# A streaming encoder step: the last 272 queries of each head as tiles of 128, 72 and 72 instead of 128, 128 and 16

## Chip, cores and metric

One core of a Trainium2 chip runs the whole step as one program. The metric is the time of one execution on the device in microseconds (us). Three runs of the kernel before took 1683.66, 1681.59 and 1683.21 us, median 1683.21. A further execution was recorded by the profiler; the rows below come from it.

## What is computed

A layer with two head groups over 2064 prompt positions (16 learned meta tokens and 2048 tokens) and a small decoding batch: normalisation, one input projection, attention with forgetting in 8 heads of 64, a gated convolution, an output projection and a last normalisation. The change touches the prompt's attention only:

```python
def fox_block(qblk, cq, qpos, k, v, ck, kpos):
    s = jnp.einsum('bqhd,bkhd->bhqk', qblk, k, preferred_element_type=jnp.float32) * (DH ** -0.5)
    s = s + jnp.transpose(cq, (0, 2, 1))[..., None] - jnp.transpose(ck, (0, 2, 1))[:, :, None, :]
    mask = kpos[None, :] <= qpos[:, None]
    s = jnp.where(mask[None, None], s, -jnp.inf)
    p = jax.nn.softmax(s, axis=-1)
    return jnp.einsum('bhqk,bkhd->bqhd', p.astype(v.dtype), v)
```

All inputs and outputs are 32-bit floats; products are made of a high and a low part of each factor.

## The kernel before

The prompt is worked in two groups of positions: 1280 first, then the other 784. For each group the kernel normalises, projects, and runs attention interleaved with projections (`ps` tiles from `hh`, `hl` and the weights `wh`, `wl`, or `wvh`, `wvl` for values) and with the convolution. At the end comes the output projection.

Attention goes by head and by unit. A unit is 256 queries, `u` from 0 to 7; units 5, 6 and 7 belong to the second group. The last one, `u` = 7, has 272 queries, since 2064 is 16 more than 8 times 256. `query_tiles` gives the query tiles of a unit as (first query, number, keys seen). A unit has three stages, each written as a generator:

- `scores_of`: for each query tile and each chunk of up to 512 keys two matmuls into `sp` (`kb,qb` with 68 rows of contraction, `ka,qa` with 128), for the last chunk a third that adds the causal mask; VectorE copies `sp` to `s` and takes the row maximum, ScalarE takes the exponential in place and the row sum into `nm`, VectorE its reciprocal.
- `weights_of`: for each block of 128 keys the weights `s` are transposed on TensorE into `tp`, one matmul per query tile with the tile's weights as the stationary and an identity as the moving operand. So a tile of 16 queries has 16 rows of contraction and 16 moving columns. ScalarE copies `tp` to `ph`, VectorE writes the rest to `pl`. `tp` has two buffers, `ph` and `pl` three. A unit of 272 has 17 key blocks: fifteen are seen by all tiles, the sixteenth by two, the last (16 keys) by one.
- `values_of`: per key block two products, `ph,vb` and `pl,vb`, into `o`; at the unit's end the reciprocals in `nm` are transposed into `tr` in the same way, one matmul per query tile, and the result is scaled and gated.

All instructions go through `Queue.call` (line 278), which notes an estimated cost in `Times`; all rows therefore carry line 278. `Times.weave` chooses, by these estimates, which generator goes on next, and this fixes the order of TensorE. On VectorE, ScalarE, GpSimd and SyncE `settle` sorts the instructions by estimated start. A transpose is booked at 109 ns whatever its columns (`cost`). `vb`, the values of a head, has one buffer; its load in `load_values` can begin when the head before has made its last product. Loads are issued on SyncE's queue (SP), stores on GpSimd's.

Of the kernel before, what the change touches and what calls it, by code (L numbers as in the profile page):

```python
# [18 lines left out]
DRAM = bass.MemoryType.DRAM  # L19

P = 128
# [11 lines left out]
NPOS = SEQ + NMETA  # L33
# [281 lines left out]
class Step:  # L315
# [4 lines left out]
        for k, v in args.items():  # L320
            setattr(self, k, v)

    def dma(self, out, in_):

        if out.dtype == F32R:
            out = out.bitcast(F32)
        if in_.dtype == F32R:
            in_ = in_.bitcast(F32)
        return getattr(self.nc, STORES if out.space == DRAM else "sync").dma_start(out=out, in_=in_)

    def open(self, ctx, name, side=None, space=None):
        k = {}
# [47 lines left out]
    def load_constants(self, pool):  # L380
        nc, dma = self.nc, self.dma
        mraw = pool.tile([P, P], F32, name="mraw")
        dma(out=mraw, in_=self.cst[:, C_MASK:C_MASK + P])
        nc.vector.tensor_copy(out=self.mask, in_=mraw)
        for i in range(3):
            dma(out=self.cw[:, :, i], in_=self.conv_w[0, i].rearrange("(c p) -> p c", p=P))

        nc.vector.tensor_scalar(out=self.cw, in0=self.cw, scalar1=0.5, scalar2=None, op0=ALU.mult)
# [22 lines left out]
    def normalise(self, ph, xp, bufs, beside=()):  # L411
# [7 lines left out]
        def prepare():  # L419
            i, (pos, rows, ct, col) = todo.pop(0)  # L420
            xt = xp.tile([P, D], F32, name="xt", bufs=bufs)
            if pos == 0:
                dma(out=xt[:NMETA], in_=self.meta_tokens)
                dma(out=xt[NMETA:], in_=self.x_p[:P - NMETA])
            else:
                dma(out=xt[:rows], in_=self.x_s if pos == NPOS else self.x_p[pos - NMETA:pos - NMETA + rows])
            if pos == p0:
                dma(out=g_bc, in_=self.norm_g[0].partition_broadcast(P))
            if beside:
                beside.pop(0)()  # L430
            sq = xp.tile([P, D], BF16, name="sq")
            ss = xp.tile([P, 1], F32, name="ss", bufs=4)
            nc.scalar.activation(out=sq[:rows], in_=xt[:rows], func=AF.Square, accum_out=ss[:rows])
            self.rsqrt(ss[:rows])
            nc.vector.scalar_tensor_tensor(out=xt[:rows], in0=xt[:rows], scalar=ss[:rows, 0:1], in1=g_bc[:rows],
                                           op0=ALU.mult, op1=ALU.mult)
            ahead.append((xt, rows, ct, col, i))
# [486 lines left out]
    @staticmethod  # L924
    def query_tiles(u):

        out = [(0, P, 256 * u + P), (P, P, 256 * u + 256)]
        return out + [(256, 16, NPOS)] if u == 7 else out

    @staticmethod  # L930
    def unit_queries(u):
# [33 lines left out]
    def scores_of(self, ph, st, ready):  # L965

        nc = self.nc
        units = st["units"]
        loaded, asked = 0, 0
        while ph not in self.summed:  # L970
            yield lambda: 0.0 if ph in self.summed else NEVER
        for n, (h, u) in enumerate(units):
            while ("q", h // 2) not in ready:
                yield lambda: 0.0 if ("q", h // 2) in ready else NEVER

            for ahead in range(2):
                if loaded < H and loaded <= h + ahead and ("k", loaded // 2) in ready:
                    self.load_head(ph, loaded)
                    loaded += 1
                if asked < len(units) and asked <= n + ahead and ("q", units[asked][0] // 2) in ready:  # L980
                    self.load_queries(ph, asked, st)
                    asked += 1
            qa, qb, ka, kb = self.qa[n % 2], self.qb[n % 2], self.ka[h % 2], self.kb[h % 2]
            done = []
            for c0, m, nk in self.query_tiles(u):
                while st["tiles"] - st["turned"] >= SB[ph]:
                    yield lambda: 0.0 if st["tiles"] - st["turned"] < SB[ph] else NEVER
                st["tiles"] += 1
                sl = self.ap.tile([P, min(self.nk, NPOS)], F32, name="s", bufs=SB[ph])
                mx = self.ap.tile([P, 8], F32, name="nm", bufs=16)  # L990
                blocks = (nk + P - 1) // P
                nch = (nk + 511) // 512
                ends = [min(nk, (blocks * (x + 1) // nch) * P) for x in range(nch)]
                k0 = 0
                for x, k1 in enumerate(ends):
                    w = k1 - k0
                    yield self.when(qa, qb, ka, kb, slot=(self.sps, "sp"))
                    sp = self.sps.tile([P, 512], F32, name="sp", bufs=SPB)
                    diag = k1 == nk
                    nc.tensor.matmul(sp[:m, :w], qb[:, c0:c0 + m], kb[:, k0:k1], start=True, stop=False)  # L1000
                    nc.tensor.matmul(sp[:m, :w], qa[:, c0:c0 + m], ka[:, k0:k1], start=False, stop=not diag)
                    if diag:
                        nc.tensor.matmul(sp[:m, w - m:w], self.identr[:, :m], self.mask[:, :m], start=False, stop=True)
                    nc.vector.tensor_scalar(out=sl[:m, k0:k1], in0=sp[:m, :w], scalar1=1.0, scalar2=None, op0=ALU.mult,
                                            op1=ALU.max, accum_out=mx[:m, x:x + 1])
                    k0 = k1
                nm = mx[:, 6:8]
                nc.vector.tensor_reduce(out=nm[:m, 0:1], in_=mx[:m, :nch], axis=AX.X, op=ALU.max, negate=True)
                nc.scalar.activation(out=sl[:m, :nk], in_=sl[:m, :nk], func=AF.Exp, bias=nm[:m, 0:1], accum_out=nm[:m, 1:2])
                nc.vector.reciprocal(out=nm[:m, 1:2], in_=nm[:m, 1:2])  # L1010
                done.append((sl, nm))
            st["scored"].append(done)
# [548 lines left out]
STORES = "gpsimd"  # L1561
# [77 lines left out]
```

## Time and profile before

| | us |
|---|---|
| median of three runs | 1683.21 |
| profiled execution | 1680.57 |
| its span in the trace | 1678.7 |
| TensorE (PE) busy | 1564.9 |
| VectorE (DVE) busy | 861.0 |
| ScalarE (ACT) busy | 632.5 |
| GpSimd (POOL) busy | 481.2 |

Times in rows are us from the span's start, durations us unless marked ns. A row of a timeline gives start, duration, engine and instruction; consecutive instructions of one kind on one tile are merged into one row with a count, under the shape of the first of them. For TensorE `16*128` are rows and columns of the stationary operand and `16x16` the moving one. TensorE's durations overlap, so the distance between two starts, not the duration, tells how long an instruction held the engine. PEld is the weight load.

### The profile page before, as it was taken

Reading aid. Unit: us, or ns where it says so; the run is one execution under the profiler, and the core shown is the slowest. Engines: PE = TensorE matmul, PEld = TensorE weight load, DVE = VectorE, ACT = ScalarE, POOL = GpSimd, SP = SyncE. Lnnn points to the kernel's source line nnn. Section 1 sums busy time; section 2 is a strip of 40 time slices with the busy share of each in tenths; the row PEclk is TensorE's granted clock in tenths of the full one; section 3 lists DMA queues with packets and bytes.
Section 4 is the critical chain, followed back from the end, with each engine's and each line's share of the span. In section 5 each row is a group of like instructions: output and inputs, shape, how many; then the busy total and the mean of one; then the engine's idle time right before and its main releaser. Section 6 shows DMA issues by size and latency. Waiting matters only on the chain.

```text
span 1678.7 us, 27726 instructions
## 1 busy us (share of the span) xinstructions
PE 1564.9 (93%) x10311; PEld 1452.5 (87%) x10311; DVE 861.0 (51%) x2276; ACT 632.5 (38%) x1196; POOL 481.2 (29%) x750
## 2 busy tenths in 40 slices
PE   4789999998999989899995999999999999999996
PEld 4779999998999978899984998998898999868885
DVE  4525667336667557552332666776576673212221
ACT  4314555325553322411111655555554553111221
POOL 2543435523211421225041313212121121223322
PEclk9899999999999998999997999999999999999998
DMA  7446653475432676522237534535534231364442
GB/s 193 118 120 158 155 142 111 113 191 139 105 77 55 219 222 194 153 53 76 40 83 155 137 101 125 127 92 158 140 67 114 37 85 31 88 232 135 142 138 88
DMA packets 159143, 206.06 MB, mean 123 GB/s; under 512 B 22220, under 2 KB 123108, under 8 KB 156320
## 3 DMA queue, kind: packets, MB, share of 16 engines
q1 hardware_dynamic: 73952, 106.38, 22.2%
q10 hardware_dynamic: 61360, 30.94, 11.9%
q0 software_dynamic: 23696, 66.96, 11.5%
q8 instruction: 82, 1.34, 0.3%
q14 instruction: 53, 0.43, 0.1%
HBM read 137.28 MB, written 66.93 MB: 122 GB/s over the span
## 4 chain that ended last, share of the span: by engine, by line
PE 73%; DMA 11%; issue 6%; POOL 3%; DVE 3%; ACT 2%; SPq 1%; ACTq 0%; POOLq 0%; DVEq 0%
PE ps L278 45%; PE sp L278 10%; PE o L278 9%; PE tp L278 8%; DMA raw<-in_w_in_dram 3%; PE tr L278 1%; DMA sqk_d<-el 1%; DMA vb<-v_d 1%; SPq L278 1%; DMA qb<-ql_d 1%; DMA cat_d<-kf 1%; DMA vn<-in_cache_v_dram 1%; DMA gz_d<-kf 1%; DMA o_d<-ol 1%; DMA xt<-in_x_prompt_dram 1%
## 5 line engine op out<-in xcount | busy, mean ns | idle before, releaser
L278 PE MATMUL ps<-hh,wh 128*128 128x256 f32 (+2 forms) x1568 | 502.0, 320 | 20.1 <-DVE el L278 10.0
L278 PE MATMUL ps<-hl,wh 128*128 128x256 f32 (+2 forms) x1568 | 486.3, 310 | 0.0
L278 PE MATMUL ps<-hh,wl 128*128 128x256 f32 (+2 forms) x1568 | 485.9, 310 | 0.0
L278 PEld LDWEIGHTS ps<-hh,wh 128*128 128x128 f32 x1568 | 302.8, 193 | 29.6 <-DVE el L278 10.6
L278 PEld LDWEIGHTS ps<-hl,wh 128*128 128x128 f32 x1568 | 302.6, 193 | 1.6
L278 PEld LDWEIGHTS ps<-hh,wl 128*128 128x128 f32 x1568 | 301.6, 192 | 0.0
L278 DVE TENSOR_TENSOR pl<-tp,ph 128x512 fp32r<-128x512 f32 (+2 forms) x360 | 198.2, 564 | 113.2 <-ACT ph L278 111.3
L278 ACT CAST ph<-tp 128x512 fp32r<-128x512 f32 (+2 forms) x360 | 170.8, 487 | 210.3 <-PE tp L278 197.3
L278 DVE TENSOR_SCALAR_CACHE_REDUCE s<-sp 128x384 f32<-128x384 f32 (+3 forms) x360 | 210.5, 598 | 35.1 <-PE sp L278 33.5
L278 ACT ACTIVATE s<-s,nm 128x128 f32<-128x128 f32 (+16 forms) x136 | 170.5, 1254 | 77.6 <-DVE nm L278 77.0
L278 PE MATMUL tp<-ident,s 128*128 128x128 f32 (+1 forms) x1224 | 191.8, 269 | 0.1
L278 PE MATMUL o<-ph,vb 128*128 128x256 f32 (+4 forms) x584 | 167.6, 306 | 3.4 <-DMA vb<-v_d 3.4
L278 PEld LDWEIGHTS tp<-ident,s 128*128 128x128 f32 (+1 forms) x1224 | 145.0, 140 | 23.9 <-issue 19.9
L278 PE MATMUL sp<-kb,qb 68*128 68x384 f32 (+3 forms) x360 | 143.2, 398 | 18.4 <-DVE s L278 10.8
L278 PE MATMUL o<-pl,vb 128*128 128x256 f32 (+4 forms) x584 | 149.6, 282 | 0.0
L278 PE MATMUL sp<-ka,qa 128*128 128x384 f32 (+3 forms) x360 | 132.7, 369 | 0.0
L278 POOL TENSOR_TENSOR gz<-gz,otmp 64x256 f32<-64x256 f32 (+1 forms) x64 | 47.2, 737 | 273.2 <-DVE otmp L278 253.7
L278 PE MATMUL ps<-o,ch 128*128 128x512 f32 x374 | 118.6, 396 | 2.0 <-DMA o<-o_d 2.0
L278 PEld LDWEIGHTS o<-ph,vb 128*128 128x128 f32 (+1 forms) x584 | 109.9, 188 | 9.1 <-DMA vb<-v_d 2.4
L278 PEld LDWEIGHTS o<-pl,vb 128*128 128x128 f32 (+1 forms) x584 | 110.5, 189 | 0.7
L278 DVE TENSOR_TENSOR wl<-raw,wh 128x1024 fp32r<-128x1024 f32 x56 | 69.0, 1232 | 63.1 <-ACT wh L278 62.4
L278 PE MATMUL ps<-wvh,hh 128*128 128x272 f32 (+3 forms) x288 | 87.2, 303 | 5.0 <-ACT sv L278 4.6
(218 smaller groups left out, 2288.2 us busy)
## 6 DMA issues: line engine op xcount, KB each, us to landing
raw<-in_w_in_dram ACTq DMA_DIRECT2D x59, 512.0 KB
cr<-cat_d SPq DMA_DIRECT2D x17, 512.0 KB
v_d<-vv POOLq DMA_DIRECT2D x32, 256.0 KB, 2.7
vb<-v_d SPq DMA_DIRECT2D x8, 1024.0 KB
oxt<-in_x_prompt_dram SPq DMA_DIRECT2D x16, 512.0 KB
out_dram<-oxt POOLq DMA_DIRECT2D x16, 512.0 KB, 2.9
xt<-in_x_prompt_dram SPq DMA_DIRECT2D x15, 512.0 KB
qa<-qh_d SPq DMA_DIRECT2D x112, 64.0 KB
```

What stands on the lines that cost most here:

```text
L278: r = f(*a, **k)
```

## The change

`query_tiles` cuts the queries of unit 7 into 128, 72 and 72. The second tile begins at query 1920 and sees 2048 keys, the third begins at 1992 and sees all 2064. Since the second tile no longer ends where its keys end, the mask matmul is given the columns from the tile's first query to the end of the chunk. `dma` gets an optional argument that nothing uses.

```diff
-    def dma(self, out, in_):
+    def dma(self, out, in_, by=None):
...
-        out = [(0, P, 256 * u + P), (P, P, 256 * u + 256)]
-        return out + [(256, 16, NPOS)] if u == 7 else out
+        if u == 7:
+            return [(0, P, 256 * u + P), (P, 72, 256 * u + 256), (200, 72, NPOS)]
+        return [(0, P, 256 * u + P), (P, P, 256 * u + 256)]
...
-                        nc.tensor.matmul(sp[:m, w - m:w], self.identr[:, :m], self.mask[:, :m], start=False, stop=True)
+                        b0 = 256 * u + c0
+                        nc.tensor.matmul(sp[:m, b0 - k0:w], self.identr[:, :m], self.mask[:, :k1 - b0], start=False, stop=True)
```

The order on TensorE in the first unit of 272, two key blocks and the start of the next; the shapes here are those of the result, partitions by columns. Before:

```order
L278 MATMUL tp<-ident,s 128x128 x2
L278 MATMUL tp<-ident,s 128x16
L278 MATMUL o<-ph,vb 128x272
L278 MATMUL o<-pl,vb 128x272
L278 MATMUL tp<-ident,s 128x128 x2
L278 MATMUL tp<-ident,s 128x16
```

And after:

```order
L278 MATMUL tp<-ident,s 128x128
L278 MATMUL tp<-ident,s 128x72 x2
L278 MATMUL o<-ph,vb 128x272
L278 MATMUL o<-pl,vb 128x272
L278 MATMUL tp<-ident,s 128x128
L278 MATMUL tp<-ident,s 128x72 x2
```

Nothing moved: each group keeps its three transposes and its place, and the widths are others. The end of the same unit, the last three key blocks, before:

```order
L278 MATMUL ps<-hh_7939,wl 128x256
L278 MATMUL tp<-ident,s 128x128 x2
L278 MATMUL tp<-ident,s 128x16
L278 MATMUL tp<-ident,s 128x128
L278 MATMUL tp<-ident,s 128x16
L278 MATMUL tp<-ident,s 16x16
L278 MATMUL sp<-kb_9563,qb_9568 128x512
```

And after:

```order
L278 MATMUL ps<-hh_7939,wl 128x256
L278 MATMUL tp<-ident,s 128x128
L278 MATMUL tp<-ident,s 128x72 x4
L278 MATMUL tp<-ident,s 16x72
L278 MATMUL sp<-kb_9563,qb_9568 128x512
```

Six transposes stand there as before, one of 128 and five of 72 columns where three of 128 and three of 16 were. SyncE's queue (SP) at the beginning of the last head, where the values `vb` (in two pieces) and the queries of the next unit (`qa`, `qb`) are loaded:

```order
+L278 DMA vb<-v_d_109 128x2048
 L278 DMA vb<-v_d_109 16x128
-L278 DMA qa_9566<-qh_d_95 64x272 x2
+L278 DMA qa_9566<-qh_d_95 64x272
+L278 DMA qb_9568<-c_d 1x2x128
+L278 DMA qa_9566<-qh_d_95 64x272
 L278 DMA qb_9568<-ql_d_99 64x272
-L278 DMA qb_9568<-c_d 1x2x128
-L278 DMA vb<-v_d_109 128x2048
 L278 DMA qb_9568<-c_d 1x2x128
```

The large piece of `vb` moved from behind four of the five query loads to the front.

## Rows read from the trace of the kernel before

**Rows 1.** The page, part 1: busy us, share of span, instructions per engine.

```profile
PE 1564.9 (93%) x10311; PEld 1452.5 (87%) x10311; DVE 861.0 (51%) x2276; ACT 632.5 (38%) x1196; POOL 481.2 (29%) x750
```

**Rows 2.** Busy times by stretch; columns as in the first line.

```profile
core 0: us, PE busy (x) PEld busy (x) DVE busy (x) ACT busy (x) POOL busy (x), PEclk, DMA share, GB/s
...
930.00:1170.00 240.00, 239.92 (x1736) 216.84 (x1735) 162.25 (x467) 130.83 (x239) 64.04 (x102) 1.00 0.45 118
1170.00:1405.00 235.00, 233.71 (x1695) 211.97 (x1694) 154.81 (x429) 121.38 (x218) 36.59 (x53) 1.00 0.38 87
```

**Rows 3.** Weight loads by shape: busy us, mean ns, idle before and its releaser.

```profile
L278 PEld LDWEIGHTS tp<-ident,s 16*128 16x128 f32 x128 | 17.1, 133 | 21.0 <-issue 19.9 <-ACT wvh L278 0.2
```

**Rows 4.** Timeline of TensorE, unit 7 of the second head: start, us, instruction.

```profile
1028.83 0.54 PE L278 MATMUL tp<-ident,s 128*128 128x128 f32 x3
1029.30 0.40 PE L278 MATMUL o<-ph,vb 128*128 128x272 f32 x1
1029.54 0.29 PE L278 MATMUL o<-pl,vb 128*128 128x272 f32 x1
...
1030.85 0.38 PE L278 MATMUL tp<-ident,s 128*128 128x128 f32 x2
```

**Rows 5.** The same group in narrower windows: from its second, its third transpose on.

```profile
1028.94 0.43 PE L278 MATMUL tp<-ident,s 128*128 128x128 f32 x2
...
1029.14 0.23 PE L278 MATMUL tp<-ident,s 16*128 16x16 f32 x1
```

**Rows 6.** Timeline of TensorE in a unit of 256 queries.

```profile
1044.54 0.61 PE L278 MATMUL tp<-ident,s 128*128 128x128 f32 x4
...
1045.11 0.29 PE L278 MATMUL o<-pl,vb 128*128 128x256 f32 x1
```

**Rows 7.** Timeline of TensorE, four transposes of 16 rows in a row.

```profile
719.18 0.41 PE L278 MATMUL sp<-ident,xt 16*128 16x16 f32 x4
719.53 0.38 PE L278 MATMUL ps<-hh,wh 128*128 128x256 f32 x1
```

**Rows 8.** Timeline of TensorE around a score matmul of 68 rows.

```profile
1012.00 0.34 PE L278 MATMUL sp<-kb,qb 68*16 68x384 f32 x1
1012.17 0.34 PE L278 MATMUL sp<-ka,qa 128*16 128x384 f32 x1
1012.35 0.28 PE L278 MATMUL ps<-wvh,hh 128*128 128x256 f32 x1
```

**Rows 9.** Timeline of TensorE: three runs of transposes and what follows them.

```profile
1017.72 1.08 PE L278 MATMUL tp<-ident,s 128*128 128x128 f32 x6
...
1018.95 0.28 PE L278 MATMUL ps<-wvl,hh 128*128 128x256 f32 x1
...
1033.70 0.99 PE L278 MATMUL tp<-ident,s 128*128 128x128 f32 x6
...
1034.96 0.40 PE L278 MATMUL sp<-ka,qa 128*128 128x512 f32 x1
...
1037.37 0.59 PE L278 MATMUL tr<-ident,nm 128*128 128x128 f32 x3
...
1038.23 0.40 PE L278 MATMUL sp<-ka,qa 128*128 128x512 f32 x1
```

**Rows 10.** Timelines of SP's issues and TensorE, start of the last head.

```profile
1348.41 0.31 SPq L278 DMA_DIRECT2D vb<-v_d  x1
...
1352.08 0.40 SPq L278 DMA_DIRECT2D vb<-v_d  x1
...
1358.02 0.36 PE L278 MATMUL o<-ph,vb 128*128 128x256 f32 x1 [1.09 <-DMA vb<-v_d]
```

**Rows 11.** Timelines of ScalarE and VectorE: copies of the group in rows 4.

```profile
1029.41 0.39 ACT L278 CAST ph<-tp 128x272 fp32r<-128x272 f32 x1 [0.80 <-PE tp L278]
...
1029.83 0.44 DVE L278 TENSOR_TENSOR pl<-tp,ph 128x272 fp32r<-128x272 f32 x1 [0.74 <-ACT ph L278]
```

More of the change, by code (lines that the diff above doesn't have):

```diff
@@ L328, in dma @@
             in_ = in_.bitcast(F32)
-        return getattr(self.nc, STORES if out.space == DRAM else "sync").dma_start(out=out, in_=in_)
+        return getattr(self.nc, by or (STORES if out.space == DRAM else "sync")).dma_start(out=out, in_=in_)
     def open(self, ctx, name, side=None, space=None):
```

## Prediction

> **What bounds the kernel now.** I read the busy shares first, then the stretch in which the changed code runs, then single rows of TensorE there, because a share says nothing about how fast an engine that is always busy could go. TensorE is busy 93% of the span [rows 1]. The units of 272 queries run between 930 and 1405 us, eight of them, one per head. In that stretch TensorE is busy 239.92 of 240 us and 233.71 of 235 us at the full granted clock (1.00, the level of 2.4 GHz), while VectorE is busy for about two thirds and ScalarE for about half [rows 2]. So a microsecond of TensorE taken out of this stretch comes off the span until another engine's result is late.
>
> What TensorE does badly there shows in the weight loads: the 128 loads with 16 rows stand behind 21.0 us of idle time, nearly all of it put down to "issue", that is, to no other engine [rows 3]. One group of three transposes shows it in order. It starts at 1028.83; the second transpose starts at 1028.94 (0.11 later), the third, with 16 rows, at 1029.14 (0.20 later), the first product `o` at 1029.30 (0.16 later), the second at 1029.54 [rows 4, 5]. From the first transpose to the second product: 0.71 us. In a unit without a 16-row tile, four transposes of 128 start at 1044.54 and the second product at 1045.11 [rows 6]: 0.57 us for one transpose more. Three steps of 0.109 (the 0.11 above, finer: 0.327 for three) leave 0.24 from the last transpose to the second product; the same stretch after a 16-row transpose is 0.40. Thus the 16-row tile costs on the way in, in itself and on the way out.
>
> Is that the price of 16 rows, or of changing to them? Four transposes of 16 rows in a row start at 719.18 and the next instruction at 719.53 [rows 7]. Take the 0.16 of the way out off these 0.35 us and three steps remain, of about 0.063 each (an estimate from these rows). So 16-row transposes are quick among themselves; the change of row count is what costs. That each of these loads 128 columns of weights also says that such a load needs no more than 0.063 us.
>
> The question is then on which side 72 rows fall. The scores have a neighbour: the matmul `sp<-kb,qb` has 68 rows and stands between matmuls of 128 rows. Its successor starts 0.17 us after it, and that one's successor 0.18 us after that, at the same 384 columns [rows 8]. No price for 68 rows on either side. I take 72 rows to behave like 68.
>
> **The change, part by part.** *Scores.* The number of score matmuls, their columns, the reductions on VectorE and the exponentials on ScalarE are the same; partitions are exchanged (128 and 16 against 72 and 72), columns are not. The mask matmul of the last tile grows from 16 to 72 columns, and the two products of the last key block do so too; with the steps of 0.109 for 128 columns as bound, each under 0.05 us, in sum under 0.15 a head. I take 0.07.
>
> *Transposes.* After the change a group is one of 128 columns (0.109) and two of 72. By columns a 72 would take 72/128 of 0.109, or 0.061; I take 0.063, the step seen above. After the last one the second product follows in 0.24 less the 0.046 by which 72 columns are shorter, 0.20 with the 16 columns more of `o`. Sum 0.109 + 0.063 + 0.20 = 0.37 against 0.71: 0.34 saved. Twelve groups of a head stand like this: 4.1 us.
>
> The other five groups of a head stand in two runs. The two triples from 1017.72 to the second matmul behind them at 1018.95 take 1.23 us; after the change 0.109 + 0.063 + 0.063 + 0.109 + 0.063 + 0.20 = 0.61, saved 0.62. The run of six from 1033.70 to 1034.96 takes 1.26 us and ends with a score matmul of 512 columns in place of 256, some 0.11 longer; after the change 0.109 + four times 0.063 + 0.30 = 0.66, saved 0.60. The three transposes of the denominators, 1037.37 to 1038.23, take 0.86 us; after it 0.109 + 0.063 + 0.30 = 0.47, saved 0.39 [rows 9]. The 16-row products of the last key block stay as they are.
>
> A head saves 4.1 + 0.62 + 0.60 + 0.39 - 0.07 = 5.6 us, eight heads 45 us.
>
> *Order.* The planner books every transpose at 109 ns whatever its columns, so around the groups its order stands still; small other costs move, and from behind the first unit of 272 on it shifts projections and scores by a few rows. The work of a head stays the same. One move has a price in the trace: in the last head the large load of `vb` now goes out ahead of four issues for `qa`/`qb`, where before it followed them, 1348.41 to 1352.08, and TensorE waited 1.09 us for it at 1358.02 [rows 10]. I credit 1 us. The other way, loads of `ka`/`kb` (five or six issues) now precede some of `qa`/`qb` in SP's queue; at 0.4 to 0.6 us an issue that is up to 3 us later for loads that are asked for one unit, some 15 us, ahead: hidden, and at most 3 us a head if not.
>
> *New waits.* `tp` has two buffers, so group j+2 may not start before VectorE has written `pl` of group j. Now ScalarE's copy starts 0.58 us after the group (1029.41), takes 0.39, VectorE's part starts 0.03 later and takes 0.44 [rows 11]: 1.44 in all; after the change the group itself is 0.14 shorter up to its last transpose (0.17 against 0.31), so 1.30, and some 0.05 for the signal. TensorE needs from group j to j+2 now 2.02 us (1028.83 to 1030.85, [rows 4]); after it 2.02 - 0.68 = 1.34. The two are equal within the reading. Where VectorE or ScalarE has something else in hand, of 0.4 us or so, the wait shows. About six such pairs a head, 48 in all: between 0 and 48 times 0.3, 14 us. I take 5 us, nearer the lower end, because the units of 128-row tiles in the same stretch run with the same two buffers and TensorE stays busy through them [rows 2].
>
> Together 45 + 1 - 5 = 41 us off. The profiled execution took 1680.57 us, its span 1678.7; I expect a span near 1638. The median of the runs is 2.6 us above the profiled one: 1683.2 - 41 = **1642 us**.
>
> **The rivals.** *A transpose of 72 columns keeps the pace of one of 128.* Then each of the 35 in a head (33 of weights, two of denominators) costs 0.046 more, 13 us in eight heads, and fewer waits appear: about 1653. The four 16-row ones [rows 7] speak against it. The Trainium skill's page "TensorE: Matmul & The Clock Gate", section "LDWEIGHTS (loading the stationary operand)", has a rule for this: loading takes the stationary columns divided by 1.2 GHz, whatever the rows. For 128 columns that is an estimate of 107 ns by that page, which would keep every transpose at the pace of 128 and give this rival's time; by it 16 rows would also cost nothing extra, and the trace has 0.063 us for such a load and 0.20 plus 0.16 around it, so the trace disagrees.
>
> *The waits decide.* If `pl` is late by 0.3 us or more at each pair because VectorE's order blocks it, the 14 us above and more are lost: 1652 to 1665.
>
> *72 rows count as another row count.* Entering costs 0.20, the second 72 follows at 0.063, leaving costs 0.40: 0.66 against 0.71, 0.05 saved some 128 times (the transposes of 16 rows, [rows 3]): about 1677. The change would then not do what its form suggests. The 68-row matmul [rows 8] speaks against it. The same skill's page "TensorEngine Tiling (Array Packing)", section "Tiling Modes", lists modes of 128, 64 and 32 rows and says that a change of mode drains the engine; 16 rows fit the mode of 32, and 72 fit only that of 128. By that rule this rival falls; the trace agrees for 68 rows.
>
> *Slower: every 72-row tile pays for itself.* If each step into and between 72-row transposes cost 0.20, a group would take 0.20 + 0.20 + 0.40 = 0.80 against 0.71, and 128 times 0.09 are 12 us: about 1695. It decides as soon as the step from 72 to 72 exceeds 0.11. No row has 72 rows; the quick run of four [rows 7] speaks against it.
>
> **How the numbers follow.** My forecast, 1634 to 1650 around 1642, has 0.80. The pace rival has 0.08, the waits 0.05, the rival of another row count 0.03, the slower one 0.04. The range reaches from all of the gain without a wait and with a slightly quicker 72 (1634) to the waits at their price (1660); beyond it lie the last two and a part of the waits. A measurement of this kernel can tell some 0.2% (3.4 us) from no change: faster 0.95, same 0.01, slower 0.04.
>
> **What would show it.** Right: from the first transpose of a group to the second product 0.37 us; the idle time put down to "issue" before weight loads of `tp` nearly gone; no row of 16 rows but those of the last key block; some 5 us per head less between the units' ends; TensorE still busy nearly throughout, with a few new waits on `pl`. Wrong: steps of 0.11 between transposes of 72 (pace), waits on `pl` or `ph` of more than 10 us in sum (waits), a gap of 0.20 ahead of each 72 (row count).

## The result, and the profile after

The changed kernel takes 1657.76 us (median of four, 1652.27 to 1664.70) against 1682.40 us of the kernel before in the same session: 0.9868 of it, 95% interval 0.9836 to 0.9900, so 24.6 us faster. The prediction had said 41 us faster. The direction holds, the size does not. The profiled execution after took 1664.70 us and its span is 1662.9; it is the slowest of the four and already 6.1 us behind the profiled execution before when the first changed instruction comes, so parts are compared below by their own lengths and not by their place on the clock.

The steps on TensorE came nearly as the sum had them. A group of the second head (timeline, first from its first transpose, then two narrower windows, as in [rows 4, 5]; start, us, instruction):

```profile
1038.00 0.40 PE L278 MATMUL tp<-ident,s 128*128 128x128 f32 x3
1038.20 0.37 PE L278 MATMUL o<-ph,vb 128*128 128x272 f32 x1
1038.41 0.29 PE L278 MATMUL o<-pl,vb 128*128 128x272 f32 x1
1038.53 0.27 PE L278 MATMUL tp<-ident,s 128*128 128x128 f32 x1
...
1038.11 0.29 PE L278 MATMUL tp<-ident,s 72*128 72x72 f32 x2
...
1038.17 0.23 PE L278 MATMUL tp<-ident,s 72*128 72x72 f32 x1
```

From 128 to 72 columns 0.11, from 72 to 72 0.06 to 0.07, from the last transpose to the first product 0.03 and to the second 0.24: 0.41 from the first transpose to the second product, where [rows 4] has 0.71. The weight loads of `tp` by shape (busy us, mean ns, idle before and its releaser) answer [rows 3]:

```profile
L278 PEld LDWEIGHTS tp<-ident,s 128*128 128x128 f32 x960 | 115.3, 142 | 13.3 <-DVE pl L278 10.0
L278 PEld LDWEIGHTS tp<-ident,s 72*128 72x128 f32 x256 | 32.5, 146 | 1.1 <-ACT s L278 1.1
```

The idle time put down to "issue", 19.9 of the 21.0 us in [rows 3], is gone. In its place the loads of 128 rows wait 10.0 us for VectorE's `pl`, where in the kernel before all loads of `tp` wait 0.3 us for it (waits: us in total, times, longest):

```profile
PEld tp L278 <- DVE pl L278: 0.3, 1, 0.3
```

The stretch of the units of 272 shows the same by its busy times (columns as in [rows 2]; x counts instructions):

```profile
936.00:1170.00 234.00, 226.66 (x1731) 215.54 (x1731) 160.84 (x463) 128.49 (x237) 63.57 (x103) 0.98 0.46 121
1170.00:1400.00 230.00, 225.12 (x1760) 215.90 (x1759) 161.07 (x446) 124.87 (x226) 37.46 (x54) 0.99 0.38 89
```

TensorE was without work for 0.08 and 1.29 us in [rows 2]; now it is for 7.34 and 4.88 us, and the granted clock is not full any more. What the weight loads waited for most in that stretch, and what ScalarE and VectorE themselves waited for among transfers:

```profile
PEld tp L278 <- DVE pl L278: 10.0, 6, 2.8
...
PEld ps L278 <- DVE kf L278: 1.7, 1, 1.7
...
ACT kf L278 <- DMA cat_d<-kf: 4.8, 1, 4.8
...
ACT ph L278 <- DMA kb<-kh_d: 4.2, 1, 4.2
ACT wvh L278 <- DMA raw<-in_w_in_dram: 3.5, 1, 3.5
...
ACT kf L278 <- DMA kb<-c_d: 1.8, 1, 1.8
...
ACT wh L278 <- DMA raw<-in_w_in_dram: 1.7, 1, 1.7
...
DVE vv L278 <- DMA v_d<-vv: 4.2, 1, 4.2
```

In the kernel before, neither ScalarE nor VectorE has a single wait on a transfer between 930 and 1405 us. Here they stand six times from the first unit of 272 on, 20.2 us in sum. (Just ahead of it ScalarE stands for the store `gz_d` in both kernels: 6.1 us before, 5.0 us after.) The longest wait of TensorE in the stretch shows how one of them travels. Timelines of SP, GpSimd, VectorE and TensorE, second head:

```profile
1021.73 0.50 SPq L278 DMA_DIRECT2D ka<-kh_d  x1
...
1022.93 0.45 SPq L278 DMA_DIRECT2D ka<-kl_d  x1
1023.42 0.60 SPq L278 DMA_DIRECT2D kb<-kh_d  x1
...
1023.06 0.76 POOL L278 DMA_DIRECT2D v_d<-vv  x1
...
1032.88 0.23 DVE L278 CAST vv<-sv 128x128 fp32r<-128x128 f32 x1 [4.20 <-DMA v_d<-vv]
1033.03 0.43 DVE L278 TENSOR_TENSOR pl<-tp,ph 128x272 fp32r<-128x272 f32 x1
...
1033.52 0.49 PE L278 MATMUL tp<-ident,s 128*128 128x128 f32 x3 [2.63 <-DVE pl L278]
```

Three loads of 516 KB for the next head's `ka` and `kb` go out within 1.7 us, and in the middle of them the store of `vv`. `vv` has two buffers, so VectorE's next copy into it stands until that store has landed. Behind it in VectorE's order is the `pl` of a finished group, and TensorE, which has two `tp`, waits for that. The issues of that microsecond (KB each, us from issue to landing), and the same line over the whole execution:

```profile
v_d<-vv POOLq DMA_DIRECT2D x1, 256.0 KB, 9.7
...
v_d<-vv POOLq DMA_DIRECT2D x32, 256.0 KB, 2.7
```

The second longest wait of TensorE, which ends at 1097.69, comes by ScalarE. It stands at its own issue of the next `raw` load, by the profile until a load of `kb` has landed, and its copies `ph` stand behind that issue:

```profile
1096.36 0.38 ACTq L278 DMA_DIRECT2D raw<-in_w_in_dram  x1
1096.78 0.67 ACT L278 CAST ph<-tp 128x272 fp32r<-128x272 f32 x2 [4.17 <-DMA kb<-kh_d]
```

Why the issue of one load waits for the landing of another was not looked into. Right behind this wait of TensorE the granted clock falls to its lower level (windows of 4 us, in the first the wait that ends at 1097.69; columns as above):

```profile
1094.00:1098.00 4.00, 1.64 (x17) 1.44 (x15) 0.79 (x2) 0.67 (x2) 0.00 (x0) 1.00 0.56 179
1098.00:1102.00 4.00, 4.00 (x25) 4.00 (x24) 2.06 (x5) 1.93 (x5) 0.54 (x1) 0.58 0.64 88
1102.00:1106.00 4.00, 4.00 (x34) 3.82 (x34) 1.76 (x5) 1.65 (x5) 0.00 (x0) 0.99 0.23 67
```

The accounts below are worked out from the traces of all kernels in the same way. The stretch runs from TensorE's instruction 5701 (just ahead of the first unit of 272) to the last product `o`, the tail from there to TensorE's end. For each instruction the usual step of its kind (by itself, its predecessor and its successor) is taken; what a step at full clock is longer by 0.06 us or more counts as a wait, what it is longer at half clock as clock.

| us | stretch | usual steps | waits | clock | rest | tail |
|---|---|---|---|---|---|---|
| before | 463.3 | 454.8 | 2.1 | 0.0 | 6.4 | 256.5 |
| after | 447.7 | 419.1 | 15.3 | 6.4 | 7.0 | 250.1 |

Stretch and tail together are 22.0 us shorter. The steps themselves give 42.1 (35.7 in the stretch and 6.4 in the tail, from which 24 instructions moved into the stretch); waits take back 13.2 and the clock 6.4.

### The profile page after: what moved, and what is told of

It reads as the page before. It is cut to its first block, busy times and chain, and to the rows that moved or that the text cites. A ratio compares the mean times of both kernels' runs of the same rounds, so it can differ in the third digit from the quotient of the medians.

```text
span 1662.9 us, 27715 instructions
## 1 busy us (share of the span) xinstructions
PE 1537.2 (92%) x10311; PEld 1449.2 (87%) x10311; DVE 862.4 (52%) x2276; ACT 630.8 (38%) x1196; POOL 479.1 (29%) x750
## 3 DMA queue, kind: packets, MB, share of 16 engines
q0 software_dynamic: 23696, 66.96, 11.6%
## 4 chain that ended last, share of the span: by engine, by line
PE 67%; DMA 15%; issue 8%; DVE 4%; POOL 3%; ACT 2%; SPq 1%; ACTq 0%; POOLq 0%; DVEq 0%
PE ps L278 43%; PE sp L278 9%; PE o L278 8%; PE tp L278 6%; DMA raw<-in_w_in_dram 3%; DMA cat_d<-kf 2%; DMA sqk_d<-el 2%; DMA vn<-in_cache_v_dram 2%; SPq L278 1%; PE tr L278 1%; DMA qb<-ql_d 1%; DMA kb<-kh_d 1%; DMA o_d<-ol 1%; DMA kb<-c_d 1%; DVE wl L278 1%
## 5 line engine op out<-in xcount | busy, mean ns | idle before, releaser
L278 PE MATMUL ps<-hh,wh 128*128 128x256 f32 (+2 forms) x1568 | 502.7, 321 | 22.4 <-DVE el L278 11.6
L278 PE MATMUL tp<-ident,s 128*128 128x128 f32 (+1 forms) x1224 | 174.9, 267 | 9.7 <-DVE pl L278 8.8
```

The costliest lines, as they stand in the source:

```text
L278: r = f(*a, **k)
```

## The experiments

**Does the row count decide, and where?** The same 144 queries as 80 and 64:

```diff
-            return [(0, P, 256 * u + P), (P, 72, 256 * u + 256), (200, 72, NPOS)]
+            return [(0, P, 256 * u + P), (P, 80, 256 * u + 256), (208, 64, NPOS)]
```

> The last 144 queries are cut into 80 and 64 instead of 72 and 72; all else as in the changed kernel. Theory that a tile below some row count pays for a change on TensorE as the 16-row tile did and that 64 is already such a count: ahead of each 64-row transpose and behind it a gap of 0.1 to 0.2 us shows, about 0.3 us a group, twelve groups and the runs in eight heads, some 30 to 45 us: 1690 to 1700. Theory that 64 rows behave as 72 and 128 do: steps of 0.06 to 0.07 us, the time of the changed kernel, 1650 to 1665.

One execution, 1684.05 us, so its rows say more than its time. A group on TensorE (timeline and two narrower windows, full clock):

```profile
959.91 0.55 PE L278 MATMUL tp<-ident,s 128*128 128x128 f32 x3
960.38 0.39 PE L278 MATMUL o<-ph,vb 128*128 128x272 f32 x1
960.61 0.29 PE L278 MATMUL o<-pl,vb 128*128 128x272 f32 x1
...
960.01 0.44 PE L278 MATMUL tp<-ident,s 80*128 80x80 f32 x2
...
960.18 0.27 PE L278 MATMUL tp<-ident,s 64*128 64x64 f32 x1
```

0.10 to the 80, 0.17 to the 64, 0.20 to the first product, 0.23 to the second: 0.70 in all, as with 16 rows. The usual steps of the stretch are 464.1 us, 45.0 more than with 72 and 72; some 5.6 of them are instructions that moved in from the tail, so the price is about 39 us. So 64 rows pay nearly the whole price of 16, and 72 and 80 pay none. The time is below the 1690 to 1700 of that theory, since the waits are 3.5 us here instead of 15.3; the half clock costs some 8 us, about as much as with 72 and 72. The Trainium skill's page "TensorEngine Tiling (Array Packing)", section "Tiling Modes", lists row modes of 128, 64 and 32 and says that changing the mode drains the engine; 64 rows fit the second, 72 only the first, and the trace agrees, with 0.29 us for a change and back.

**Is it the moved order?** The planner is made to book VectorE's, ScalarE's and GpSimd's pieces of 72 columns as pieces of 16, which leaves the orders of TensorE, VectorE and GpSimd as they were before the change:

```diff
             cols *= x
+        if queue != "tensor" and cols == 72:
+            cols = 16
```

> The changed tiles (128, 72, 72), but the planner books the two small copies that grew (16 to 72 columns) at their old price, so that TensorE, VectorE and GpSimd keep the order of the kernel before; the price of a transpose is untouched. Theory A (pace: the faster groups of transposes use up the time in which ScalarE and VectorE could wait for a transfer, whatever the order): about 1657 us, as the changed kernel, with 15 to 25 us more of lost TensorE time between 930 and 1400 us than before, in waits on pl and in the half clock behind them. Rival B (order: the planner's shifted rows put ScalarE's and VectorE's instructions behind transfers by chance): about 1642 us, with under 10 us lost there.

1658.27 us (1655.19 to 1664.40), no different from the changed kernel; waits 14.8, clock 6.1. The order that the change moves on these three engines is not the cause. On SP's queue 75 of 648 instructions still stand elsewhere than in the kernel before, so the share of the loads' order is not settled by this run.

**Is it TensorE's pace?** One transpose of 128 columns more ahead of each group of the first fifteen key blocks, unseen by the planner, and then three:

```diff
                 for j, rows, c0, at in grp:
+                    for _ in range(3 if u == 7 and j < 15 else 0):
+                        self.nc.tensor.engine.transpose(out=tp[:rows, at:at + P], in_=done[0][0][:P, j * P:j * P + rows],
+                                                        identity=self.ident)
```

> The changed kernel with one more transpose of 128 columns, not booked by the planner, at the head of each of the 120 groups of three: its result is written over by the next, so it only takes TensorE 0.109 us a group, 13 us in sum. Theory A (waits come from the pace): a part of the 13 us falls into waits that then shrink, 1660 to 1665 us, with fewer and shorter waits on pl. Rival B (waits stand where they are): 1670 us, with the waits as long as before.

> Three more transposes of 128 columns, not booked by the planner, ahead of each of the 120 groups of the first fifteen key blocks; order as in the changed kernel. 3 times 0.109 makes 0.33 us a group, about what a group was shorter than before: TensorE is back at its old pace while its order, the queues and the loads stay. 39 us of added work. Theory that the old pace covered the late copies: the 15 us of waits and the 6 us of half clock go back to about 2 and 0, so 1657.8 + 39 - 19 = 1678 (1672 to 1684). Rival, that the waits come with the new order and the place of the loads whatever the pace, as one filler a group suggests (it cost 13.9 of its 13 us): 1657.8 + 39 = 1697 (1690 to 1702).

One filler: 1671.71 us, 13.9 more than the changed kernel for 13 us of work. Waits 12.4, clock 3.2: the profile gives a little back, the times nothing. Three: 1689.05 us (1686.49 to 1691.79), 31.3 more for 39 us; waits 6.7, clock 1.6. That lies between the two expectations and outside both ranges. The old pace did cover stands, but at its full dose ScalarE and VectorE still stand, 15.5 us in sum:

```profile
ACT wvh L278 <- DMA raw<-in_w_in_dram: 4.4, 1, 4.4
ACT kf L278 <- DMA cat_d<-kf: 4.2, 1, 4.2
ACT ph L278 <- DMA kb<-kh_d: 2.9, 1, 2.9
...
ACT kf L278 <- DMA kb<-c_d: 1.0, 1, 1.0
...
DVE vv L278 <- DMA v_d<-vv: 3.0, 1, 3.0
```

Waits and clock together go from 21.7 us to 8.3, and not to the 2.1 of the kernel before. Pace is one condition, then, and not the source. Whether the rest comes from the changed order of the queues, which stands here, or from the fillers' place ahead of the group was not separated.

**Is it the transfers?** In the second group the loads of `ka`, `kb` (from its third head on) and `vb` (from its second) fetch a sixteenth of their rows; the rest of the tile keeps an earlier head's values, so the attention of these heads is not the reference's. They are booked in full, and the orders of TensorE, VectorE and ScalarE stand still. Once in the changed kernel, once in the kernel before:

```diff
-        self.dma(out=vb[:, :full], in_=v[:, h % 4, :full])
+        self.load_part(ph == 1 and h >= 1, vb[:, :full], v[:, h % 4, :full])
```

> In the second group the loads of ka and kb from the third head on, and of vb from the second head on, fetch only a sixteenth of their rows (the rest stays as an earlier head left it); they are booked in full, so the order of TensorE, VectorE and ScalarE is that of the changed kernel. About 2.5 MB a head less. Theory that ScalarE and VectorE stand because stores and weight loads land late among these loads: their stands on v_d, cat_d, gz_d and kb shrink, TensorE's waits in the stretch go from 15 to 6 us or less, the half clock from 6 to 2 or less: 1640 to 1648. Rival, that the stands don't hang on the loads: 1654 to 1661.

> The kernel before (128, 128 and 16) with the same loads cut to a sixteenth of their rows as in the experiment on the changed kernel, order kept. It is the other half of that comparison. Theory that the loads cost something only where the queries are cut into 72 and 72, since the slower TensorE of before had hidden them: 1678 to 1683, no different from the kernel before, so that with these loads out the change is worth the 40 us forecast. Rival, that the loads cost some 17 us in any kernel: 1660 to 1666.

The changed kernel falls to 1640.83 us (1637.99 to 1642.75), the kernel before stays at 1677.73 (0.9995 of the original, 0.9970 to 1.0019). Both came as the theory of late transfers had them. In the changed kernel the waits of ScalarE and VectorE on stores and on `kb` are gone from the stretch; the two on `raw` are left. No wait of TensorE there is over 0.9 us, and the clock stays at its full level:

```profile
ACT wvh L278 <- DMA raw<-in_w_in_dram: 3.5, 1, 3.5
...
ACT wh L278 <- DMA raw<-in_w_in_dram: 1.4, 1, 1.4
...
PE tp L278 <- ACT s L278: 0.9, 1, 0.9
...
930.00:1160.00 230.00, 228.72 (x1790) 218.05 (x1789) 166.68 (x480) 132.03 (x243) 63.66 (x103) 1.00 0.34 88
1160.00:1390.00 230.00, 229.09 (x1812) 220.41 (x1811) 159.40 (x435) 124.20 (x226) 42.36 (x61) 1.00 0.28 58
```

Most of the waits that remain (3.6 us in the table below) stand between 961 and 978 us, in the first head, behind those two; the `ka` and `kb` of the first two heads are loaded in full. Between these two kernels the change is worth 36.9 us, or 38 by their ratios to the kernel before, since each was timed in another session.

**Can the planner or another queue mend it?** Transposes booked by their columns; besides that, transfers booked as landing 2 us later; and, by itself, the weight tiles `raw` issued on SP instead of ScalarE:

```diff
-                return 109.0
+                return max(64.0, cols * 109.0 / 128)
...
-DMA_LATENCY = 1000.0
+DMA_LATENCY = 3000.0
...
-    def fetch_w(self, queue="scalar"):
+    def fetch_w(self, queue="sync"):
```

> The changed kernel, but the planner books a transpose by its columns (109 ns for 128, 64 for 72 or fewer) instead of 109 for all, so it plans the pace that TensorE has. Theory A: waits on pl become shorter because more other matmuls stand between the groups: 1645 to 1652 us. Rival B or waits that are set by transfers alone: 1655 to 1660 us, no better than the changed kernel.

> Transposes booked by their columns as in the experiment that did this alone (1649.6), and besides a transfer booked as landing 3 us after its packets instead of 1 us. Theory that the rest of the waits comes from transfers that land later than booked: the 7.6 us of waits left go to 4 or less, 1642 to 1647. Rival, that the place of the stands is only moved: 1647 to 1656.

> The changed kernel with the loads of projection weights (raw) issued from SyncE's queue instead of ScalarE's. If ScalarE's standing at such an issue, 3.7 us at 1092.6 and 2 us at two later places of the changed kernel, is what delays ph and pl: 4 to 8 us faster, about 1651 us, and no wait of ScalarE on a load of kb. If stores into kf and vv buffers are the cause: same as the changed kernel, 1657 us, or slower by a few us where SyncE's queue now stands at these issues.

The first alone gives 1649.58 us (0.9803 of before, 0.9773 to 0.9833), as its theory of shorter waits had it: waits 7.6, clock 1.6. With late landings as well it gives 1660.77, slower than either expectation: waits 21.8, of which 12.9 for `vb` by the waits of TensorE (PE):

```profile
PE o L278 <- DMA vb<-v_d: 12.9, 3, 8.2
PE tp L278 <- DVE pl L278: 5.5, 4, 2.2
```

A planner that sees transfers as later put others on the path; its theory falls. `raw` on SP costs: 1722.79 us, far beyond both expectations. Some 54 us are lost ahead of the stretch, where TensorE's waits for `vb` are 24.9 us instead of 2.7 and those for `qb` 18.7 instead of 7.2; within the stretch the waits stay at 14.2. So moving `raw` to SP is no remedy. What ScalarE's stands at its issues of `raw` cost by themselves this run does not tell, since all the queues changed with it.

**Spreading the loads.** The three loads of the next head go out one at each of the head's three units instead of all at its first; in the second group only, same bytes:

```diff
         dma(out=ka[0:DH, :npos], in_=self.kh_d[p][rows, :npos])
+        yield
         dma(out=ka[DH:P, :npos], in_=self.kl_d[p][rows, :npos])
+        yield
         dma(out=kb[BR:, :npos], in_=self.kh_d[p][rows, :npos])
...
-                    self.load_head(ph, loaded)
-                    loaded += 1
+                    list(head)
+                    head = self.load_head(ph, loaded)
+                    loaded += 1
+                    if not ahead or ph == 0:
+                        list(head)
...
+            next(head, None)
             qa, qb, ka, kb = self.qa[n % 2]
```

> The changed kernel, whose loads of the next head's ka (two) and kb (one with its sums), in the second group, go out one at each of the head's three units instead of all at its first. Same bytes. Theory that the stands come from stores and weight loads that land behind this burst of 1.5 MB: fewer stands, TensorE's waits from 15 to 8 or less, 1645 to 1652. Rival, that any place of these loads hits some store or that the moved order costs as much: 1654 to 1662.

> The kernel before (128, 128 and 16) with the same loads spread over a head's three units. In the changed kernel the spreading gave 31 us, 21 of them in the stretch of the units of 272 (waits and half clock) and about 10 at the start of the second group, 900 to 930 us, where the burst of two heads' loads stood before the first scores of both kernels. Theory that only the 10 us are to be had in the kernel before, whose slow TensorE hid the rest: 1665 to 1670, and with the loads spread the change is worth some 40 us, the size forecast. Rival, that the spreading pays the same in both: 1645 to 1650.

> Both: loads spread over the three units and transposes booked by their columns (1649.6 alone). If the two act on different waits: 1640 to 1646. If on the same ones: 1646 to 1652.

The changed kernel with spread loads takes **1626.97 us** (1622.86 to 1631.45; 0.9688 of before, 0.9660 to 0.9717), 18 us less than the better of its two expectations allowed, and beats both kernels. Of the 30.8 us against the changed kernel 20.6 lie in stretch and tail, the rest ahead of the stretch. TensorE is busy through the stretch again, and ScalarE and VectorE wait only for `raw` there:

```profile
915.00:1145.00 230.00, 230.00 (x1810) 220.40 (x1810) 171.17 (x492) 136.16 (x249) 65.13 (x104) 1.00 0.52 135
1145.00:1375.00 230.00, 228.37 (x1814) 220.68 (x1813) 155.92 (x424) 120.79 (x221) 43.56 (x63) 1.00 0.38 86
...
PE o L278 <- DMA vb<-v_d: 1.6, 1, 1.6
...
ACT wh L278 <- DMA raw<-in_w_in_dram: 1.6, 2, 1.0
```

The kernel before with spread loads takes 1668.13 us (0.9927, 0.9899 to 0.9956), as its theory had it: 11.6 us are gained ahead of the stretch, at the start of the second group, and 4.5 in stretch and tail, 3.6 of them in the usual steps. Between these two the change is worth 41.2 us, 40 by their ratios.

| us | stretch | usual steps | waits | clock | rest | tail |
|---|---|---|---|---|---|---|
| before, part loads | 461.4 | 454.8 | 0.2 | 0.0 | 6.5 | 257.9 |
| after, part loads | 429.7 | 419.1 | 3.6 | 0.0 | 7.0 | 250.9 |
| before, spread | 470.6 | 463.0 | 1.0 | 0.0 | 6.7 | 244.7 |
| after, spread | 427.3 | 418.7 | 2.1 | 0.0 | 6.5 | 249.9 |

Spreading moves TensorE's order too, so how much of its gain comes from the thinner traffic and how much from the new order was not separated; the stores do not land sooner by their medians (`v_d` 4.7 us against 2.7 in the stretch). Booking by columns and spreading together give 1650.37, no better than the first alone: three waits for `vb`, 11.4 us, come back. The planner's order is not robust, and each version has to be measured.

## Why the prediction was right in direction and wrong in size

*What bounds the kernel* held: TensorE's steps in the stretch set the end.

*Transposes and scores* held. A group takes 0.41 where 0.37 was forecast: the step from 72 to 72 is 0.066 instead of 0.063, and the second product follows the last transpose in 0.237 instead of 0.20, as after a transpose of 128. With 0.30 for 0.34 in twelve groups, 45 us become 41; the account has 42.1. [rows 8] show only the way out of 68 rows; the step into it, 1011.88 to 1012.00, is 0.12 like the one before it, so that reading holds. The rivals of the pace and of the row count fell with the same rows, and the split at 64 shows the second one's price in full, only at another row count.

*Order* held as far as it was tested: the kernel with the order of TensorE, VectorE and GpSimd kept takes the same time, and TensorE waits for no `vb` in the stretch now, where [rows 10] has 1.09 us (that credit is contained in the 13.2 below).

*New waits* is the step that failed: 5 us taken, 19.6 measured (13.2 of waits and 6.4 of clock). The calculation followed one chain, `tp` to `ph` to `pl`, with the durations of [rows 11], and asked whether that chain is quick enough. It is: with the loads cut, the weight loads of `tp` wait 0.2 us for `pl` in all. It did not ask what else stands in the queues of ScalarE and VectorE ahead of these copies. Its reason for a low figure was that TensorE stays busy through the units of 128-row tiles with the same two `tp`; that TensorE never waits there held at the pace of the kernel before, where nothing in those queues waits for a transfer. Two buffers of `vv` and of `kf`, one of `raw`, and a burst of 1.5 MB a head fitted with little to spare; with TensorE 8% quicker in the stretch, copies come to a buffer while its store is still in flight. The rows of a kernel that never waits do not show how near it is to waiting. That most of the copies are late because of the loads of `ka`, `kb` and `vb` is shown by the two kernels with part of the loads; how much of it the pace brings and how much the order of the loads is not shown.

The bound of 14 us for this term was therefore no bound: it counted 48 waits of 0.3 us, and what came were about twenty waits, five of them of 1.2 to 2.8 us. The second part, the clock, was left out of the sum altogether; [rows 2] has it at 1.00 before, and no wait there was longer than 1.3 us. Steps of 42.1 less 19.6 make 22.5 us, near the 24.6 of the medians; two comparisons without late transfers give 36.9 and 41.2. That the last is the 41 forecast is chance, since the forecast holds 5 us of waits and this pair has almost none.

*The rivals.* "The waits decide" came true in its time (1652 to 1665), though not by its mechanism. The prediction's last paragraph named waits on `pl` of more than 10 us as the sign of it, and 10.0 is what the weight loads show. The prediction says that its range reaches to the waits at their price, 1660, but the range that it states ends at 1650; the measured time lies between the two.

## What to carry to other kernels

A transpose of 16 or of 64 rows between ones of 128 cost about 0.3 us here for the change and the way back, and one of 72 cost nothing, so a remainder is better shared out than left small. When the engine that sets the end is made quicker, list for every other queue the transfers that it stands for and the buffers behind them, not only the chain that feeds that engine; their slack is part of what is being spent. And when a gain goes missing, cut the suspected transfers in both kernels with the order kept: the pair says at once what the change is worth without them.

## What the runs showed of the hardware that was not expected

The price of a row count has its edge between 64 and 72 rows: 80 to 64 rows 0.17 us and back 0.43 to the second product, against 0.07 and 0.24 with 72. After a 72-row transpose the first product starts 0.03 us later and the second only 0.21 us after that.

Waits of TensorE cost more than their length: behind three of 2.1 to 2.8 us its granted clock was at half (0.58 over 4 us in one case), and once behind a run of waits of which none was longer than 0.72 us; 13.7 us at half in the stretch, and 6.4 us of time. The length of the wait does not tell how much follows: with 80 and 64 rows a wait of 1.3 us at 1023.6 us was followed by 20 us at half (0.51 from 1025 to 1045 us).

A store of 256 KB issued among three loads of 516 KB took 9.7 us to land, against a median of 2.7. The Trainium skill's page "DMA: Bandwidth & Descriptors", section "Queues, rings and completion order", says that each transfer engine takes turns between the queues that have work for it; a store would then share with the loads, not stand behind all of them. The trace agrees: between 1024 and 1030 us, with this store in flight, the loads' queue moved 1.20 MB and the stores' queue 0.39 MB.
